# Two transformer blocks on one core: a planner that lets certain DVE and POOL instructions exclude each other, and convolution sums kept in PSUM

## The chip, the cores and the metric

The kernel runs on one core of a Trainium2 chip. The metric is the device time of the whole program in microseconds. The engines are named as in the profile: PE (TensorE, matrix products; PEld its weight loads), DVE (VectorE), ACT (ScalarE), POOL (GpSimd) and SP (SyncE, which issues the DMAs).

## The reference

Sequence of 512 tokens, width 1024, float32, batch 1. Two blocks follow each other, each with two layers:

```python
def first_block(x, ...):                       # twice:
    h = _rmsnorm(x, g_mix[l]); p = h @ w_in[l]
    # latent attention, 8 heads of 64+32, with rotary tables
    y_attn = _mla_attention(q_nope, q_rope, k_nope, k_rope, v)
    a, gt = jnp.split(p[..., o3:], 2, axis=-1)
    u = a * jax.nn.sigmoid(gt)                 # 512 channels
    u = _dwconv(u, w_dw_conv[l], b_dw_conv[l]) # 31 taps over the tokens
    u = jax.nn.silu(_layernorm(u, ...))
    x = x + jnp.concatenate([y_attn, u], axis=-1) @ w_o[l]
    z = _dwconv(_rmsnorm(x, g_ffn[l]) @ w_up[l], w_dw_ffn[l], b_dw_ffn[l])   # 3 taps
    zg, zv = jnp.split(z, 2, axis=-1)
    x = x + (jax.nn.silu(zg) * zv) @ w_down[l]
def second_block(x, p, ...):
    # layer 0: state space mixer; layer 1: gated linear recurrence; each followed by
    # layer norms, a squared-relu feed-forward (4096 wide) and an embedding gate
```

## The kernel before

Everything is kept transposed: a tile has 128 channels in its partitions and the 512 tokens in its columns, so x is eight tiles. Weights come from HBM in units (128 columns of eight row tiles are the usual one, 512 KB) into one of three buffers of class `r`. Each unit is split exactly into two float32r parts: `hi`, a cast that ACT or DVE makes, and `lo`, the remainder, a subtraction (`s<-r,s` in the profile) that DVE or POOL makes. An operand is split the same way, and each product is three float32r products (hi*hi, hi*lo, lo*hi) into a PSUM bank.

No order is written by hand. `record` runs through the program and only notes each operation with the tiles that it reads and writes; `schedule` then plays the core through with a cost for every operation (`cost`, `cost_tensor`) and latencies between engines, picks at each step the operation and the engine that can start first (ties by `prio`), and gives each tile a buffer; `issue` emits the instructions in that order. Each engine then works through its own list in order. Since all instructions are emitted by one line of `issue`, the profile gives all of them that line (L572 before). Tile classes stand in the profile's names: `psum` (eight banks), `s` (86 buffers of 2 KB a partition), `r` weights, `u` the padded inputs of the convolutions, `V` small vectors such as taps, `t` and `n` small tiles, `C` constants.

Some operations may go to either of two engines: `R.either` is POOL first, DVE second, `R.other` the reverse, `copy` ACT first, DVE second. In `schedule` the second choice pays `second` (2000) in the priority and is only considered if it would end no more than `eager` (500 ns) after the first. `KEEP` says how many buffers of a class an operation must leave for older operations that have yet to take theirs; for `psum` it is 2.

`mixer1` is the mixer of block 1: `in0`/`in1` (norm, projections, gates U, latents, rope tables in layer 0), then eight heads of attention and, after each second head, `conv_tile(j)` for one of four channel tiles, then the output projection. A convolution tile has 31 taps. DVE takes 17 of them, each one instruction U * tap + sum; for 14 taps (`SIDE_TAPS`) ACT makes the product and `R.either` adds it to a second sum; a last `R.either` addition joins the two:

```python
R.vector.scalar_tensor_tensor(conv[j], U[j][:, k:k + S], wc, conv[j], op0=ALU.mult, op1=ALU.add)
...
R.scalar.activation(t, U[j][:, k:k + S], AF.Identity, scale=vec(f"w_dw_conv{l}", j * CONV_K + k))
...
R.either.tensor_add(side, side, t)
...
R.either.tensor_add(conv[j], conv[j], side)
```

Of the kernel before, what the change touches and what calls it, by code (L numbers as in the profile page):

```python
# [14 lines left out]
ALU = mybir.AluOpType  # L15
# [23 lines left out]
# ---------------------------------------------------------------- weight units  # L39
def weight_units():  # L40
    """(name, layer, first row, row tiles, column pieces); a piece is (start, stop) or (None, zeros)."""
# [100 lines left out]
# ---------------------------------------------------------------- small vectors  # L142
def vec_layout():
    """name -> (first column, columns)"""
# [64 lines left out]
def constants():  # L209
    """[128, *] of 0 and 1: identity, s<=l, all ones, rope sum, two-way selector, level masks"""  # L210
# [19 lines left out]
# ---------------------------------------------------------------- recorded program and its schedule  # L230
class Tl:
    """A tile of the recorded program; its memory is chosen when the program is scheduled."""
# [11 lines left out]
class Ap:  # L244
    """An access pattern on a recorded tile: the steps to rebuild it and the elements it covers."""
# [68 lines left out]
class Op:  # L314
    __slots__ = ("i", "eng", "calls", "cost", "preds", "succs", "npred", "ready", "tiles", "start", "end", "prio", "label", "tab", "tail", "bias", "alts", "done")


class Recorder:
    """Takes the instructions in program order, orders them per engine by a simulation of the core, and issues them."""
# [8 lines left out]
    def __init__(self):  # L328
        self.ops, self.bias, self.label, self.switch = [], 0, "", 150
        self.greed, self.order_w, self.second, self.eager = 0.015, 1.0, 2000, 500  # L330
# [34 lines left out]

    def cost_tensor(self, calls):
        """A product streams its columns while the weights of the next one load."""
        stream, load = [], []
        for meth, args, kw in calls:
            n, m = args[0].n, args[1].n  # L370
            once = meth == "transpose" or args[1].tl.dt == F32R
            stream += [2.5 + n / 2.4] if once and meth != "transpose" else [2.5 + n / 1.2] * (1 if once else 2)
# [3 lines left out]
    def together(self, calls):  # L376
        """Products of the tensor engine that stay in one run."""
        self.add("tensor", "matmul", (), {}, [("matmul", a, k) for a, k in calls])

    def any(self, *forms):  # L380
        """One operation in several forms (engine, method, arguments, options); the schedule picks one."""
        eng, meth, args, kw = forms[0]
        self.add(eng, meth, args, kw)
        self.ops[-1].alts = [(e, self.cost(e, m, a, k), [(m, a, k)]) for e, m, a, k in forms]

# [1245 lines left out]
```

## Time and profile before

| | |
|---|---|
| time, median of 3 runs | 2938.12 us (2937.53 to 2942.33) |
| profiled execution | span 2940.1 us, first to last instruction, 2.0 us above that median; no other time of it is given |
| busy | PE 2778.7 us, DVE 2051.8, POOL 1459.2, ACT 1193.5 |
| DMA | 230.74 MB read, 79 GB/s over the span |
| mean granted clock of PE | 0.977 |

A row of a group gives what it writes and reads, the shape, the count, then busy us and mean ns of one instruction, then the engine's idle time before them and who ended it. A row of a stretch gives its length, then for PE, PEld, DVE, ACT and POOL the busy us (and instructions), the granted PE clock, the share of the DMA engines' time, and GB/s. A row of the timeline gives start, length, engine and instruction, merged over equal neighbours. A row of the waits gives who waited for whom: us in total, times, longest.

### The profile page before, as it was taken

The numbers are of one execution on the slowest core, as the hardware profiler recorded it, in microseconds if no ns is written. First come the engines' busy times: TensorE is split into PE (matmuls) and PEld (weight loads), VectorE is DVE, ScalarE is ACT, GpSimd is POOL, SyncE is SP. The second block draws the span as 40 slices with busy tenths as digits, with TensorE's granted clock in tenths as the row PEclk, the third lists the DMA queues.
The fourth block names the chain that finished last, engine by engine and source line by source line (L and its number), as shares of the span: only waits on it lengthen the run. The fifth ranks groups of instructions, "written<-read, shape, count | busy, mean of one in ns | idle before, by whom it ended". The sixth has DMA issues, their size and how long they took to land. (4 is left out here: it accounts for less than half of the span.)

```text
span 2940.1 us, 37496 instructions
## 1 busy us (share of the span) xinstructions
PE 2778.7 (95%) x14054; PEld 2283.6 (78%) x14054; DVE 2051.8 (70%) x2962; ACT 1193.5 (41%) x2162; POOL 1459.2 (50%) x1163
## 2 busy tenths in 40 slices
PE   7788999999788999999999999999989999899999
PEld 5566788888577888887667888888878788788888
DVE  8999777766998766675674665455687777745546
ACT  4585332335584332244553333122345563322223
POOL 5786434454875334462254563344564544434443
PEclk8899999999899999999999999999999999999999
DMA  4003213331013223331112422233231113223230
GB/s 161 13 24 122 72 65 108 115 126 35 9 58 115 72 100 94 102 108 37 37 44 79 124 70 95 92 106 109 64 94 44 51 51 99 75 93 108 94 108 30
DMA packets 69445, 235.26 MB, mean 80 GB/s; under 512 B 7824, under 2 KB 11024, under 8 KB 69264
## 3 DMA queue, kind: packets, MB, share of 16 engines
q1 hardware_dynamic: 69264, 232.87, 24.7%
q8 instruction: 111, 1.82, 0.2%
q14 instruction: 70, 0.57, 0.1%
HBM read 230.74 MB, written 2.10 MB: 79 GB/s over the span
## 5 line engine op out<-in xcount | busy, mean ns | idle before, releaser
L572 PE MATMUL psum<-s,s 128*128 128x512 f32 (+2 forms) x12752 | 2709.8, 370 | 73.1 <-DVE s L572 49.7
L572 PEld LDWEIGHTS psum<-s,s 128*128 128x128 f32 (+1 forms) x12752 | 2167.4, 190 | 521.8 <-DVE s L572 62.5
L572 POOL TENSOR_TENSOR s<-r,s 128x512 fp32r<-128x512 f32 (+1 forms) x632 | 894.1, 1434 | 903.6 <-ACT s L572 452.0
L572 POOL TENSOR_TENSOR s<-s,s 128x512 f32<-128x512 f32 (+4 forms) x395 | 468.3, 1201 | 379.0 <-DVE s L572 215.5
L572 ACT CAST s<-r 128x512 fp32r<-128x512 f32 (+1 forms) x681 | 385.4, 609 | 381.8 <-DMA r<-wts 340.1
L572 DVE TENSOR_TENSOR s<-s,s 128x512 fp32r<-128x512 f32 (+4 forms) x453 | 418.3, 935 | 84.9 <-ACT s L572 70.1
L572 DVE TENSOR_TENSOR s<-s,psum 128x512 f32<-128x512 f32 (+2 forms) x400 | 224.6, 590 | 284.0 <-PE psum L572 283.2
L572 DVE SCALAR_TENSOR_TENSOR s<-u,V,s 128x512 f32<-128x512 f32 x304 | 324.1, 1076 | 52.5 <-ACT s L572 49.1
L572 ACT ACTIVATE s<-s 128x512 f32<-128x512 f32 (+1 forms) x338 | 188.8, 578 | 281.5 <-DVE s L572 279.5
L572 ACT ACTIVATE s<-psum 128x512 f32<-128x512 f32 (+2 forms) x174 | 91.5, 527 | 453.3 <-PE psum L572 449.1
L572 ACT ACTIVATE s<-u,V 128x512 f32<-128x512 f32 x200 | 144.3, 760 | 258.2 <-DVE u L572 257.8
L572 DVE TENSOR_TENSOR s<-r,s 128x512 fp32r<-128x512 f32 (+1 forms) x237 | 235.7, 1010 | 12.9 <-ACT s L572 9.3
L572 PE MATMUL psum<-C,s 128*128 128x128 f32 (+1 forms) x500 | 93.2, 282 | 53.2 <-POOL s L572 26.4
L572 DVE SCALAR_TENSOR_TENSOR s<-psum,s 128x512 f32<-128x512 f32 (+1 forms) x88 | 55.7, 638 | 112.1 <-ACT s L572 112.1
L572 DVE CAST s<-r 128x512 fp32r<-128x512 f32 (+1 forms) x188 | 101.3, 554 | 42.3 <-DMA r<-wts 42.2
L572 PEld LDWEIGHTS psum<-C,s 128*128 128x128 f32 x500 | 66.3, 157 | 73.0 <-POOL s L572 27.9
L572 DVE CAST s<-s 128x512 fp32r<-128x512 f32 (+1 forms) x105 | 105.8, 1008 | 8.1 <-POOL s L572 2.9
L572 DVE TENSOR_TENSOR u<-psum,s 128x512 f32<-128x512 f32 x88 | 60.5, 687 | 71.1 <-PE psum L572 70.7
L572 ACT CAST s<-s 128x512 fp32r<-128x512 f32 (+2 forms) x110 | 63.4, 587 | 99.8 <-DVE s L572 86.8
L572 ACT ACT_TABLE_LOAD x70 | 89.8, 1283 | 17.7 <-DVE s L572 14.2
L572 DVE SCALAR_TENSOR_TENSOR s<-psum,V,s 128x511 f32<-128x511 f32 (+4 forms) x90 | 66.4, 745 | 38.7 <-ACT s L572 32.9
L572 DVE TENSOR_TENSOR s<-psum,s 128x512 fp32r<-128x512 f32 (+3 forms) x131 | 84.8, 678 | 3.8 <-PE psum L572 2.1
(85 smaller groups left out, 1052.7 us busy)
## 6 DMA issues: line engine op xcount, KB each, us to landing
r<-wts SPq DMA_DIRECT2D x415, 512.0 KB, 3.6
r<-wts SPq DMA_DIRECT2D x12, 256.0 KB, 2.7
r<-wts SPq DMA_DIRECT2D x8, 384.0 KB, 3.0
s<-xT SPq DMA_DIRECT2D x8, 256.0 KB, 5.8
s<-pT SPq DMA_DIRECT2D x8, 256.0 KB, 4.0
outT<-s SPq DMA_DIRECT2D x16, 128.0 KB, 1.7
r<-wts SPq DMA_DIRECT2D x9, 128.0 KB, 2.1
V<-vecs SPq DMA_DIRECT2D x1, 480.5 KB, 6.7
```

What stands on the lines that cost most here:

```text
L572: getattr(eng, meth)(*[res(a) for a in args], **{k: res(v) for k, v in kw.items()})
```

## The change

Five things change in the planner and one in the program.

- `shares` marks operations that the planner from now on treats as needing one common port: every POOL operation, and DVE operations with two large inputs outside PSUM, or a copy or tensor_scalar from and to SBUF. `schedule` starts a marked operation no earlier than the end of the last marked one (`port`).
- The rule for the second engine is replaced: `second` and `eager` are 0, and an operation on the slower of its engines is counted as starting later by half the difference of the two costs (`drag`).
- A float32r product of n columns is planned at 2.5 + n/2.28 ns, before 2.5 + n/2.4.
- `KEEP["psum"]` is 4, before 2.
- The running sum of a convolution tile is a PSUM bank, and the last addition is always DVE's, from that bank to SBUF.
- Comments and docstrings are gone, so line numbers differ (`issue` emits at L590 now).

```diff
-        self.greed, self.order_w, self.second, self.eager = 0.015, 1.0, 2000, 500
+        self.greed, self.order_w, self.second, self.eager, self.drag = 0.015, 1.0, 0, 0, 0.5
...
+    @staticmethod
+    def shares(eng, meth, args, kw):
+        if eng != "vector":
+            return eng == "gpsimd"
+        out = kw["out"] if "out" in kw else args[0]
+        ins = list(args if "out" in kw else args[1:]) + [v for n, v in kw.items() if n not in ("out", "accum_out")]
+        near = sum(isinstance(a, Ap) and a.n > 1 and a.tl.cls != "psum" for a in ins)
+        if meth in ("tensor_scalar", "tensor_copy"):
+            return near == 1 and out.tl.cls != "psum"
+        return near > 1
...
-            stream += [2.5 + n / 2.4] if once and meth != "transpose" else [2.5 + n / 1.2] * (1 if once else 2)
+            stream += [2.5 + n / 2.28] if once and meth != "transpose" else [2.5 + n / 1.2] * (1 if once else 2)
...
-                    s = max(t0, s)
+                    s = max(t0, s, port) if o.shared[p] else max(t0, s)
...
+                    s += self.drag * ([x[1] for x in o.alts if x[0] == p][0] - min(x[1] for x in o.alts))
                     key = (s, o.prio + (self.switch if load else 0) + (self.second if p != o.alts[0][0] else 0), o.i)
...
+                if o.shared[p]:
+                    port = o.end
...
-KEEP = {"psum": 2, "s": 18, "u": 2, "t": 6, "n": 16}
+KEEP = {"psum": 4, "s": 18, "u": 2, "t": 6, "n": 16}
...
         def conv_tile(j):
             R.label = f"conv{l}"
+            acc = bank()
             for k in range(CONV_K - SIDE_TAPS):
                 wc = vec(f"w_dw_conv{l}", j * CONV_K + k)
                 if k == 0:
-                    R.vector.tensor_scalar(conv[j], U[j][:, 0:S], wc, vec(f"b_dw_conv{l}", j), op0=ALU.mult, op1=ALU.add)
+                    R.vector.tensor_scalar(acc, U[j][:, 0:S], wc, vec(f"b_dw_conv{l}", j), op0=ALU.mult, op1=ALU.add)
                 else:
-                    R.vector.scalar_tensor_tensor(conv[j], U[j][:, k:k + S], wc, conv[j], op0=ALU.mult, op1=ALU.add)
+                    R.vector.scalar_tensor_tensor(acc, U[j][:, k:k + S], wc, acc, op0=ALU.mult, op1=ALU.add)
...
-                R.either.tensor_add(conv[j], conv[j], side)
+            R.vector.tensor_add(conv[j], acc, side)
```

The change reorders the whole program, so three places of the new order are shown. In the program as a whole POOL has 1163 instructions before and 714 after, DVE 2962 and 3370, ACT 1996 and 2037 (without table loads and the like). Of the subtractions `s<-r,s` with 512 columns, POOL has 618 before and 357 after, DVE 230 and 491.

The start of the convolution of layer 0 on DVE; `u2` and `u0` are inputs of two channel tiles, `V0` holds the taps. Before:

```order
L572 SCALAR_TENSOR_TENSOR s52_623<-u2_71,V0_65,s52_623 128x512
L572 SCALAR_TENSOR_TENSOR s62_629<-u0_67,V0_65,s62_629 128x512
L572 SCALAR_TENSOR_TENSOR s52_623<-u2_71,V0_65,s52_623 128x512
L572 SCALAR_TENSOR_TENSOR s62_629<-u0_67,V0_65,s62_629 128x512
L572 SCALAR_TENSOR_TENSOR s52_623<-u2_71,V0_65,s52_623 128x512
L572 SCALAR_TENSOR_TENSOR s68_775<-psum1_658,V0_65,s70_766 128x512
```

and after:

```order
L590 SCALAR_TENSOR_TENSOR psum2_617<-u2_71,V0_65,psum2_617 128x512
L590 TENSOR_SCALAR psum0_877<-u0_67,V0_65 128x512
L590 SCALAR_TENSOR_TENSOR psum2_617<-u2_71,V0_65,psum2_617 128x512
L590 SCALAR_TENSOR_TENSOR psum0_877<-u0_67,V0_65,psum0_877 128x512
L590 TENSOR_SCALAR n5_899<-psum7_883 128x4
L590 SCALAR_TENSOR_TENSOR s83_904<-psum5_747,V0_65,s50_893 128x512
L590 SCALAR_TENSOR_TENSOR psum2_617<-u2_71,V0_65,psum2_617 128x512
L590 SCALAR_TENSOR_TENSOR psum0_877<-u0_67,V0_65,psum0_877 128x512
```

The sums are in banks 2 and 0, two at a time, and instructions of the latents and the attention stand between the steps that before stood in a block.

The first subtractions of weights on POOL, ahead of its part of the first norm (`n3_531`, `n2_515`: a power of four columns). Before:

```order
L572 TENSOR_TENSOR s84_461<-r1_406,s81_450 128x512
L572 TENSOR_TENSOR s28_480<-r2_424,s5_472 128x512
L572 TENSOR_TENSOR s33_514<-r0_465,s31_507 128x512
L572 TENSOR_TENSOR n3_531<-n2_523,n0_74 128x4
L572 TENSOR_TENSOR s38_545<-r0_465,s9_505 128x512
```

and after:

```order
L590 MEMSET u3_80 128x15 x2
L590 ISA
L590 TENSOR_TENSOR n2_515<-n1_505,n0_74 128x4
L590 TENSOR_TENSOR s41_544<-r2_448,s34_480 128x256
L590 TENSOR_TENSOR s43_551<-r0_466,s38_490 128x256
```

Nothing but memsets stands ahead of the power on POOL now; the subtractions are on DVE.

The same norm on DVE: `n2_523` and `n1_505` are made from the sums that PE left in bank 7; `s54`, `s55` and `s62`, `s63` belong to the rope tables. Before:

```order
L572 TENSOR_SCALAR s55_299<-s55_299 128x512
L572 TENSOR_SCALAR s54_295<-s54_295,V0_65 128x512
L572 CAST s31_507<-r0_465 128x512
L572 SCALAR_TENSOR_TENSOR s11_512<-s83_456,V0_65,s54_295 128x512
L572 TENSOR_SCALAR s55_299<-s55_299,V0_65 128x512
L572 TENSOR_SCALAR n2_523<-psum7_509 128x4
```

and after:

```order
L590 SCALAR_TENSOR_TENSOR s62_332<-s66_348,s62_332 128x512
L590 SCALAR_TENSOR_TENSOR s63_338<-s78_403,s63_338 128x512
L590 TENSOR_SCALAR n1_505<-psum7_498 128x4
L590 SCALAR_TENSOR_TENSOR s62_332<-s77_398,s62_332 128x512
L590 SCALAR_TENSOR_TENSOR s63_338<-s33_473,s63_338 128x512
L590 TENSOR_TENSOR n3_528<-n2_515 128x4
```

Before, nearly all of the rope tables' work stood ahead of the norm; now part of it stands behind.

More of the change, by code (lines that the diff above doesn't have):

```diff
@@ L314 @@
 class Op:
-    __slots__ = ("i", "eng", "calls", "cost", "preds", "succs", "npred", "ready", "tiles", "start", "end", "prio", "label", "tab", "tail", "bias", "alts", "done")
+    __slots__ = ("i", "eng", "calls", "cost", "preds", "succs", "npred", "ready", "tiles", "start", "end", "prio", "label", "tab", "tail", "bias", "alts", "done", "shared")
 class Recorder:
@@ L384, in any @@
         self.ops[-1].alts = [(e, self.cost(e, m, a, k), [(m, a, k)]) for e, m, a, k in forms]
+        self.ops[-1].shared = {e: self.shares(e, m, a, k) for e, m, a, k in forms}
     def add(self, eng, meth, args, kw, calls=None):
@@ L392, in add @@
             o.alts = [(e, self.cost(e, meth, args, kw), calls) for e in self.EITHER.get(eng, (eng,))]
+        o.shared = {e: eng != "tensor" and self.shares(e, meth, args, kw) for e, _, _ in o.alts}
         eng = o.alts[0][0]
@@ L471, in schedule @@
         order = []
-        table, loads = None, 0
+        table, loads, port = None, 0, 0.0
         while n < len(ops):
@@ L522, in schedule @@
             (s, _, _), o, p = best
+            o.eng, o.cost, o.calls = [x for x in o.alts if x[0] == p][0]
+            s -= self.drag * (o.cost - min(x[1] for x in o.alts))
             o.start = s
-            o.eng, o.cost, o.calls = [x for x in o.alts if x[0] == p][0]
             for e, _, _ in o.alts:
@@ L960, in conv_tile @@
                 if k == 0:
-                    R.vector.tensor_scalar(conv[j], U[j][:, 0:S], wc, vec(f"b_dw_conv{l}", j), op0=ALU.mult, op1=ALU.add)
+                    R.vector.tensor_scalar(acc, U[j][:, 0:S], wc, vec(f"b_dw_conv{l}", j), op0=ALU.mult, op1=ALU.add)
                 else:
-                    R.vector.scalar_tensor_tensor(conv[j], U[j][:, k:k + S], wc, conv[j], op0=ALU.mult, op1=ALU.add)
-            if SIDE_TAPS:
-                side = None
-                for k in range(CONV_K - SIDE_TAPS, CONV_K):
-                    t = tl()
-                    R.scalar.activation(t, U[j][:, k:k + S], AF.Identity, scale=vec(f"w_dw_conv{l}", j * CONV_K + k))
-                    if side is None:
-                        side = t
-                    else:
-                        R.either.tensor_add(side, side, t)
-                R.either.tensor_add(conv[j], conv[j], side)
+                    R.vector.scalar_tensor_tensor(acc, U[j][:, k:k + S], wc, acc, op0=ALU.mult, op1=ALU.add)
+            side = None
+            for k in range(CONV_K - SIDE_TAPS, CONV_K):
+                t = tl()
+                R.scalar.activation(t, U[j][:, k:k + S], AF.Identity, scale=vec(f"w_dw_conv{l}", j * CONV_K + k))
+                if side is None:
+                    side = t
+                else:
+                    R.either.tensor_add(side, side, t)
+            R.vector.tensor_add(conv[j], acc, side)
         att = [pair() for _ in range(4)]
```

## Prediction, made before the changed kernel ran

> **What bounds the kernel now.** I read the page's first block, then the busy time of stretches of the span, because the average hides that the limit changes from stage to stage.
>
> ```profile
> span 2940.1 us, 37496 instructions
> ...
> PE 2778.7 (95%) x14054; PEld 2283.6 (78%) x14054; DVE 2051.8 (70%) x2962; ACT 1193.5 (41%) x2162; POOL 1459.2 (50%) x1163
> ```
>
> ```profile
> core 0: us, PE busy (x) PEld busy (x) DVE busy (x) ACT busy (x) POOL busy (x), PEclk, DMA share, GB/s
> 50.00:250.00 200.00, 146.62 (x710) 116.96 (x710) 198.58 (x277) 133.10 (x257) 155.81 (x114) 0.90 0.11 37
> 350.00:700.00 350.00, 350.00 (x1534) 287.59 (x1533) 237.15 (x285) 107.77 (x178) 151.31 (x113) 1.00 0.28 95
> 705.00:925.00 220.00, 189.37 (x873) 151.32 (x872) 211.91 (x297) 150.45 (x286) 164.57 (x122) 0.91 0.16 51
> 950.00:1250.00 300.00, 300.00 (x1314) 246.64 (x1313) 204.85 (x252) 89.38 (x143) 116.51 (x80) 1.00 0.29 92
> 2150.00:2500.00 350.00, 323.38 (x2363) 283.43 (x2362) 258.20 (x403) 180.68 (x340) 172.46 (x158) 0.97 0.21 65
> ```
>
> 350 to 700 and 950 to 1250 are the feed-forward layers of block 1: PE is never idle, DVE has 30% left. No order of instructions makes them shorter, since PE's own rate sets it (1093 products in 250.6 us, 0.229 us each):
>
> ```profile
> L572 PE MATMUL psum<-s,s 128*128 128x512 f32 x1093 | 250.6, 392 | 0.0
> ```
>
> 50 to 250 and 705 to 925 are the two mixers with attention and the 31-tap convolution. There DVE is busy 198.6 of 200 and 211.9 of 220 us, PE idles 53.4 and 30.6 us. So DVE sets the time of these 420 us, and what DVE does in them is the question. Its groups in the two mixers (the first four rows from 50 to 250, the last three from 705 to 875), and behind them groups of the whole span that read PSUM:
>
> ```profile
> L572 DVE SCALAR_TENSOR_TENSOR s<-u,V,s 128x512 f32<-128x512 f32 x64 | 78.2, 1258 | 0.0
> L572 DVE CAST s<-r 128x512 fp32r<-128x512 f32 x15 | 12.1, 823 | 0.0
> L572 DVE TENSOR_TENSOR s<-s,s 128x512 f32<-128x512 f32 x9 | 11.1, 1240 | 0.0
> L572 DVE TENSOR_TENSOR s<-r,s 128x512 fp32r<-128x512 f32 x7 | 6.2, 890 | 0.0
> ...
> L572 DVE SCALAR_TENSOR_TENSOR s<-u,V,s 128x512 f32<-128x512 f32 x64 | 72.2, 1139 | 0.2
> L572 DVE TENSOR_SCALAR s<-u,V 128x512 f32<-128x512 f32 x4 | 5.0, 1256 | 0.0
> L572 DVE TENSOR_SCALAR s<-u,V 128x512 f32<-128x512 f32 x4 | 5.0, 1263 | 0.0
> ```
>
> ```profile
> L572 DVE TENSOR_TENSOR s<-s,psum 128x512 f32<-128x512 f32 x256 | 169.2, 681 | 241.2 <-PE psum L572 240.6
> L572 DVE SCALAR_TENSOR_TENSOR s<-s,V,psum 128x512 f32<-128x512 f32 x32 | 22.8, 743 | 15.9 <-PE psum L572 15.0 <-POOL s L572 0.8
> ...
> L572 DVE SCALAR_TENSOR_TENSOR s<-psum,V,s 128x511 f32<-128x511 f32 x24 | 17.9, 748 | 33.0 <-ACT s L572 32.9
> ```
>
> A convolution step (U times a tap plus the running sum, both in SBUF) takes 1.258 us, the same form with one operand in PSUM 0.743. The timeline tells why. DVE's and POOL's rows around 90 and 108 us:
>
> ```profile
> 88.68 15.38 DVE L572 SCALAR_TENSOR_TENSOR s<-u,V,s 128x512 f32<-128x512 f32 x9
> 108.31 4.05 DVE L572 SCALAR_TENSOR_TENSOR s<-u,V,s 128x512 f32<-128x512 f32 x6
> ...
> 89.87 15.32 POOL L572 TENSOR_TENSOR s<-s,s 128x512 f32<-128x512 f32 x9
> 113.08 0.13 POOL L572 MEMSET u<- 128x1 f32 x2 [7.89 <-DVE s L572]
> ```
>
> While POOL adds, nine steps take nine POOL times (1.71 us each); while POOL stands still (the 7.89 us before 113.08), six take 4.05 us, 0.675 each. The two engines alternate: an instruction of the one runs only when that of the other is through. DVE instructions with a PSUM operand show no trace of it.
>
> **The change, part by part.** (a) The running sums move to PSUM. 64 steps in each mixer leave the alternation. No row has DVE writing a 512-column PSUM tile, so the price is bounded: below by the 0.675 of a step without POOL, above by the 1.258 of now (no gain at all). I take 0.675, since the nearest rows (0.743 and 0.748, durations that overlap the next instruction by some 0.07, as six of 0.74 fit into 4.05) show no surcharge for a PSUM input. Layer 0: 64 x (1.258 - 0.675) = -37.3 us of DVE. Layer 1: 64 x (1.139 - 0.675) = -29.7. The first step of a tile (TENSOR_SCALAR, 1.26) gives 4 x 0.58 = -2.3 in each.
>
> [...]
>
> (b) Fewer instructions on POOL. Counted in the program, POOL goes from 1163 to 714 and DVE from 2962 to 3370; the mixer of layer 0 has 136 on POOL before and 95 after, 358 and 399 on DVE; that of layer 1 137 and 113, 316 and 333. What goes over is mostly the second half of the weight split (s<-r,s). Alone on DVE it takes 0.68 us, less the overlap 0.61, and a cast 0.42:
>
> ```profile
> 55.04 0.68 DVE L572 TENSOR_TENSOR s<-r,s 128x512 fp32r<-128x512 f32 x1
> ...
> 59.84 0.42 DVE L572 CAST s<-r 128x512 fp32r<-128x512 f32 x1
> ```
>
> Layer 0: 41 x 0.61 = 25 us more for DVE, of which some 20 in the stretch where it is full (before 50 us DVE has idle time: the 41 include the splits of the first weights). Layer 1: 17 x 0.61 = +10.4.
>
> (c) With less on POOL, the other DVE instructions wait less. Layer 0, by the rows above: casts 15 x (823 - 420) = 6.0 us, adds 9 x (1240 - 680) = 5.0, splits 7 x 0.21 = 1.5; -12.5 at most. Layer 1 has 12 such adds, -6.7. POOL still has 95 and 113 instructions, so I count three quarters: -9.4 and -5.0.
>
> (d) PE's waits. In 50 to 250 it waited 31.2 us for POOL and 15.4 for DVE:
>
> ```profile
> PE psum L572 <- POOL s L572: 17.8, 3, 16.6
> PE psum L572 <- DVE s L572: 15.4, 13, 3.6
> PE psum L572 <- POOL n L572: 13.4, 1, 13.4
> ```
>
> The 13.4 ends at 63.66: all banks hold products that wait for the row factor of the first norm; its DVE part (62.25, in n<-psum) stood behind the angle reduction of the rope tables. The 16.6 ends at 117.13, a sum on POOL behind the adds above.
>
> ```profile
> 44.59 9.59 DVE L572 SCALAR_TENSOR_TENSOR s<-s,s 128x512 f32<-128x512 f32 x14
> 62.25 0.15 DVE L572 TENSOR_SCALAR n<-psum 128x4 f32<-128x4 f32 x1
> ...
> 63.66 1.11 PE L572 MATMUL psum<-C,n 128*128 128x128 f32 x4 [13.44 <-POOL n L572]
> 117.13 0.59 PE L572 MATMUL psum<-C,s 128*128 128x1 f32 x2 [16.63 <-POOL s L572]
> ```
>
> Both lie within the stretch that DVE fills and are how its lateness reaches PE; they are not added. In the new order the norm's instruction stands ahead of a dozen of the rope's, the convolution is spread between the attention's instructions, and the side adds remain on POOL, so both waits should shrink by more than half.
>
> (e) The rest. PE's price in the planner (512 columns: 227 ns, before 216) agrees with the 0.229 above and makes no product faster. The feed-forward stages take 46 more DVE instructions in layer 0, 46 x 0.61 = 28 us into the 113 that DVE has free there: nothing. ACT gets 39 more casts, 39 x 0.6 = 24 us at 41% busy: nothing. The recurrence (2150 to 2500) is a chain of DVE and PE; DVE gets 78 more instructions (29 of 0.61, the rest, mostly of 256 columns, about 0.37: +36 us) and loses waits, by the first three rows below against 412 for 256 columns (the fourth, which reads PSUM) and 680 for 512: 64 x 0.40 + 57 x 0.24 + 31 x 0.36 = -50 at most.
>
> ```profile
> L572 DVE TENSOR_TENSOR s<-s 128x256 f32<-128x256 f32 x64 | 48.8, 811 | 0.0
> L572 DVE TENSOR_TENSOR s<-s,s 128x256 f32<-128x256 f32 x57 | 35.8, 655 | 1.1 <-POOL s L572 0.9
> L572 DVE TENSOR_TENSOR s<-r,s 128x512 fp32r<-128x512 f32 x31 | 31.8, 1038 | 1.9 <-ACT s L572 1.5
> ...
> L572 DVE TENSOR_TENSOR s<-s,psum 128x256 f32<-128x256 f32 x128 | 46.7, 412 | 23.7 <-PE psum L572 23.5
> ...
> L572 ACT CAST s<-r 128x512 fp32r<-128x512 f32 (+1 forms) x681 | 385.4, 609 | 381.8 <-DMA r<-wts 340.1
> 130.00:250.00 120.00, 98.54 (x517) 78.25 (x517) 118.95 (x186) 88.76 (x180) 102.64 (x78) 0.97 0.12 42
> ```
>
> With three quarters of that it is a wash: 0, between -15 and +15.
>
> Sum: layer 0: -37.3 - 2.3 + 20 - 9.4 = -29.0. Layer 1: -29.7 - 2.3 + 10.4 - 5.0 = -26.6. Together -55.6, so 2940.1 - 55.6 = 2884.5 for the profiled execution. Its span stands 2.0 above the median of the runs (2938.1); the forecast is 2882.5, rounded 2883.
>
> **Rivals.** *PE takes over at once, larger gain.* If spreading the convolution ends DVE's lateness altogether, both stretches shrink to PE's busy time: 53.4 + 30.6 = 84, 2854; and the clock there (0.90, 0.91) would be granted in full as in the stages without holes, up to 10% of the 336 busy us, so down to about 2830. For: ACT and POOL have room. Against: DVE still needs some 170 of 200 us in each, and attention goes back and forth.
>
> *The banks run out, slower.* An accumulator holds one of eight banks for 17 steps, and two are open at once (order on DVE, above); six are left. The planner now keeps four for older work, up from two, so a later head can start only with five free. From the point where just one half-head is in flight, each of its four visits to DVE queues behind a convolution step: 16 x 4 x 0.675 = 43 us a layer against the 28 gained, +15 each, about 2968. For: attention already fills 130 to 250 us (the last row above) with DVE at 118.95. Against: in the new order PE's rows of the attention still change between several heads' tiles, as before. [...]
>
> *PSUM writes are slow.* At the upper end of (a) the 39.6 and 32.0 us are lost, and the sum is -55.6 + 71.6 = +16: 2954.
>
> *No change.* What DVE saves on waits (12.5 + 39.6 in layer 0) it gives back on moved work and new stalls; then 2938. It needs moved work to cost double (41 x 1.26 = 52), the price it has only beside a busy POOL.
>
> **How the numbers follow.** Forecast 0.56, larger gain 0.25, no change 0.06, slow PSUM writes 0.03, banks 0.10. A difference of 0.2% (6 us) is about what can be told from no change here. Faster 0.81, same 0.06, slower 0.13. The range takes in the larger gain down to 2832 and, upward, losing half the sum (2910) and a recurrence 15 us worse (2925); left out are most of the last three cases, 0.19.
>
> **What would show it.** Right: convolution steps at 0.74 us whatever POOL does; POOL near 900 us busy, DVE's s<-r,s mean below 0.85; feed-forward starting some 29 us earlier in layer 0 and 56 in layer 1; PE's waits for POOL before 250 us under 15. Wrong: steps above 0.9 us; PE idle within the feed-forward stages; attention stretches longer than 120 us, PE waiting for DVE in them; the time from 2150 to 2500 growing.

## The result and the profile after

The changed kernel takes 2814.4 us (median; 2811.9 to 2816.2), the one before, run beside it, 2939.8: a ratio of 0.957 (95% interval 0.956 to 0.959), 125 us less. The direction was predicted, the size was not: 2883 was forecast, and 2814 lies below the range. The first block of the page of after:

```profile
span 2814.0 us, 37098 instructions
...
PE 2745.5 (98%) x14054; PEld 2259.6 (80%) x14054; DVE 1923.5 (68%) x3370; ACT 1215.0 (43%) x2201; POOL 837.1 (30%) x714
```

PE is now busy for all but 68 us of the span, against 161 before, and its products are 33 us shorter in sum, while the granted clock rose from 0.977 to 0.993. DVE does 408 more instructions in 128 us less.

Where the time went, by stages of the program. A stage begins with the first product of it in the trace (matched to the order of products in the program), so the rows of one column can be compared, although nothing in the trace is labelled. "ssd" is the state space mixer and "recurrence" the gated linear one; ff is each stage's feed-forward (with gate and tail). One profiled execution each, us:

| kernel | mixer 0 | ff 0 | mixer 1 | ff 1 | ssd | ff, gate | recurrence | ff, tail |
|---|---|---|---|---|---|---|---|---|
| before | 296.8 | 367.8 | 258.0 | 377.1 | 436.5 | 422.9 | 342.5 | 438.6 |
| after | 259.2 | 366.1 | 233.0 | 368.3 | 425.1 | 422.3 | 307.5 | 432.5 |
| difference | -37.6 | -1.7 | -25.0 | -8.9 | -11.3 | -0.6 | -34.9 | -6.1 |

Half of the gain is in the two mixers of block 1 (-62.6), where it was predicted (-55.6, though two of its terms were off in opposite directions, as is told below). A second large piece is in the recurrence, for which 0 was predicted. The busy time of stretches of after, columns as in the prediction; the first and third are the mixers, the second and fourth their feed-forward, the last is the recurrence:

```profile
50.00:250.00 200.00, 175.01 (x841) 136.65 (x842) 189.34 (x328) 158.99 (x298) 128.77 (x107) 0.97 0.18 61
259.00:625.00 366.00, 366.00 (x1593) 298.10 (x1592) 245.48 (x360) 124.58 (x202) 66.70 (x56) 1.00 0.29 99
667.00:858.00 191.00, 177.37 (x858) 140.97 (x857) 174.59 (x309) 152.82 (x289) 122.39 (x104) 0.97 0.19 59
858.00:1227.00 369.00, 367.67 (x1650) 301.45 (x1648) 251.25 (x391) 126.97 (x211) 62.59 (x47) 1.00 0.30 99
2074.00:2381.00 307.00, 304.99 (x2331) 271.88 (x2330) 233.06 (x469) 186.29 (x352) 85.29 (x77) 1.00 0.22 71
```

From 50 to 250 us PE gets through 841 products where it did 710, at a clock of 0.97 instead of 0.90, and DVE is still nearly full (189 of 200): the mixers have become shorter, not another kind of stage. In the recurrence it is otherwise: PE is busy 305.0 of 307 us. Before, its whole stretch was

```profile
2159.00:2501.00 342.00, 315.38 (x2331) 277.04 (x2331) 250.48 (x398) 176.86 (x332) 165.54 (x155) 0.97 0.20 62
```

26.6 us of holes, and 10.4 us more for the same 2331 products at the lower clock. All but 2.0 us of holes is gone, 35 us together.

DVE's groups of after from 50 to 250 us (two rows), from 667 to 858 (the next) and in the whole span:

```profile
L590 DVE SCALAR_TENSOR_TENSOR psum<-u,V,psum 128x512 f32<-128x512 f32 x64 | 47.3, 742 | 0.3
L590 DVE TENSOR_TENSOR s<-s,s 128x512 f32<-128x512 f32 x18 | 15.9, 882 | 0.7 <-ACT s L590 0.7
...
L590 DVE SCALAR_TENSOR_TENSOR psum<-u,V,psum 128x512 f32<-128x512 f32 x64 | 45.7, 742 | 0.1
...
L590 DVE TENSOR_TENSOR s<-r,s 128x512 fp32r<-128x512 f32 x491 | 346.9, 733 | 5.4 <-ACT s L590 3.5
```

A convolution step takes 0.742 us (1.258 and 1.139 before) while POOL is busy 129 and 122 us of these stretches. What PE waited for from 50 to 250 us, and where the two waits stand that the prediction named:

```profile
PE psum L590 <- ACT s L590: 12.6, 18, 2.1
PE psum L590 <- DVE s L590: 10.0, 10, 2.3
PE psum L590 <- POOL n L590: 2.6, 1, 2.6
```

```profile
50.56 0.65 PE L590 MATMUL psum<-C,n 128*128 128x128 f32 x4 [2.59 <-POOL n L590]
```

Of 31.2 us waiting for POOL, 2.6 are left. The first norm's factor comes at 50.56 instead of 63.66, and the wait of 16.6 us for a sum on POOL no longer exists.

### The profile page after: what moved, and what is told of

It is laid out like the page before. It is cut to its first block, busy times and chain, and to the rows that moved or that the text cites. A ratio compares the mean times of both kernels' runs of the same rounds, so it can differ in the third digit from the quotient of the medians.

```text
span 2814.0 us, 37098 instructions
## 1 busy us (share of the span) xinstructions
PE 2745.5 (98%) x14054; PEld 2259.6 (80%) x14054; DVE 1923.5 (68%) x3370; ACT 1215.0 (43%) x2201; POOL 837.1 (30%) x714
## 4 chain that ended last, share of the span: by engine, by line
PE 82%; DVE 13%; issue 3%; ACT 2%; POOL 0%; DMA 0%; DVEq 0%; POOLq 0%; ACTq 0%; SPq 0%
PE psum L590 82%; DVE s L590 9%; DVE psum L590 2%; ACT s L590 2%; DVE n L590 1%; ACT L590 0%; DMA r<-wts 0%; POOL s L590 0%; DVE u L590 0%; POOL n L590 0%; POOL u L590 0%; DVEq L590 0%; POOLq L590 0%; ACTq L590 0%; SPq L590 0%
## 5 line engine op out<-in xcount | busy, mean ns | idle before, releaser
L590 PE MATMUL psum<-s,s 128*128 128x512 f32 (+3 forms) x12752 | 2676.4, 368 | 36.5 <-DVE s L590 22.4
L590 PEld LDWEIGHTS psum<-s,s 128*128 128x128 f32 (+1 forms) x12752 | 2147.8, 188 | 480.1 <-DVE s L590 38.7
L590 POOL TENSOR_TENSOR s<-r,s 128x512 fp32r<-128x512 f32 (+1 forms) x370 | 498.0, 1363 | 1085.0 <-ACT s L590 696.0
L590 ACT CAST s<-r 128x512 fp32r<-128x512 f32 (+1 forms) x708 | 404.2, 610 | 374.1 <-DMA r<-wts 353.5
L590 DVE TENSOR_TENSOR s<-s,s 128x512 f32<-128x512 f32 (+5 forms) x610 | 402.4, 679 | 78.9 <-ACT s L590 68.4
L590 DVE TENSOR_TENSOR s<-s,psum 128x512 f32<-128x512 f32 (+2 forms) x400 | 224.5, 591 | 309.8 <-PE psum L590 309.3
L590 POOL TENSOR_TENSOR s<-s,s 128x512 f32<-128x512 f32 (+5 forms) x230 | 265.0, 1163 | 571.2 <-DVE s L590 352.5
L590 DVE TENSOR_TENSOR s<-r,s 128x512 fp32r<-128x512 f32 (+1 forms) x499 | 349.9, 728 | 5.4 <-ACT s L590 3.5
L590 ACT ACTIVATE s<-s 128x512 f32<-128x512 f32 (+1 forms) x338 | 187.7, 578 | 233.5 <-DVE s L590 230.9
L590 ACT ACTIVATE s<-psum 128x512 f32<-128x512 f32 (+2 forms) x174 | 91.7, 528 | 412.2 <-PE psum L590 409.6
L590 ACT ACTIVATE s<-u,V 128x512 f32<-128x512 f32 x200 | 142.9, 761 | 274.1 <-DVE u L590 273.8
L590 DVE SCALAR_TENSOR_TENSOR s<-u,V,s 128x512 f32<-128x512 f32 x176 | 146.1, 831 | 49.4 <-ACT s L590 47.1
L590 DVE SCALAR_TENSOR_TENSOR s<-psum,s 128x512 f32<-128x512 f32 (+1 forms) x88 | 55.6, 639 | 119.1 <-ACT s L590 119.1
L590 DVE TENSOR_TENSOR u<-psum,s 128x512 f32<-128x512 f32 x88 | 60.6, 689 | 89.1 <-PE psum L590 89.1
L590 PE MATMUL psum<-C,s 128*128 128x128 f32 (+1 forms) x500 | 87.1, 277 | 19.1 <-ACT s L590 14.2
L590 ACT CAST s<-s 128x512 fp32r<-128x512 f32 (+2 forms) x121 | 70.6, 592 | 64.7 <-DVE s L590 63.7
L590 DVE CAST s<-r 128x512 fp32r<-128x512 f32 (+1 forms) x161 | 68.7, 441 | 39.3 <-DMA r<-wts 39.3
L590 DVE TENSOR_TENSOR s<-psum,s 128x512 fp32r<-128x512 f32 (+4 forms) x139 | 90.7, 679 | 7.0 <-ACT s L590 6.4
L590 POOL TENSOR_TENSOR n<-n,n 128x4 f32<-128x4 f32 (+1 forms) x32 | 34.4, 1076 | 204.7 <-DVE n L590 204.4
L590 DVE SCALAR_TENSOR_TENSOR psum<-u,V,psum 128x512 f32<-128x512 f32 x128 | 93.0, 742 | 0.5
L590 PEld LDWEIGHTS psum<-C,s 128*128 128x128 f32 x500 | 61.3, 149 | 36.1 <-ACT s L590 22.4
## 6 DMA issues: line engine op xcount, KB each, us to landing
r<-wts SPq DMA_DIRECT2D x12, 256.0 KB, 2.8
s<-xT SPq DMA_DIRECT2D x8, 256.0 KB, 6.0
s<-pT SPq DMA_DIRECT2D x8, 256.0 KB, 4.0
```

Of the source, the lines that this page charges most:

```text
L590: getattr(eng, meth)(*[res(a) for a in args], **{k: res(v) for k, v in kw.items()})
```

## The experiments

Times are medians against the kernel before in the same runs, with the ratio's interval. Stages in us, of one profiled execution each:

| run | time | ratio (95%) | mixer 0 | mixer 1 | ssd | recurrence |
|---|---|---|---|---|---|---|
| before | 2939.8 | 1 | 296.8 | 258.0 | 436.5 | 342.5 |
| after | 2814.4 | 0.957 (0.956 to 0.959) | 259.2 | 233.0 | 425.1 | 307.5 |
| e1 PSUM sums alone | 2886.9 | 0.982 (0.980 to 0.984) | 272.6 | 235.4 | 436.9 | 342.1 |
| e2 rule alone | 2947.3 | 1.003 (1.002 to 1.004) | 305.0 | 270.4 | 435.2 | 340.1 |
| e3 rule and port | 2855.6 | 0.971 (0.970 to 0.973) | 280.8 | 251.4 | 428.9 | 304.4 |
| e4 all but PSUM | 2853.8 | 0.971 (0.969 to 0.972) | 272.0 | 256.0 | 426.5 | 306.8 |
| e5 rule, POOL priced dear | 2904.1 | 0.988 (0.986 to 0.990) | 286.7 | 268.4 | 438.7 | 316.3 |
| e6 all but the port | 2910.7 | 0.991 (0.989 to 0.992) | 291.8 | 254.0 | 436.7 | 333.3 |
| e7 port, not in recurrence | 2841.6 | 0.967 (0.965 to 0.968) | 259.9 | 232.0 | 425.2 | 335.6 |
| e8 port with old rule | 2928.7 | 0.996 (0.995 to 0.998) | 312.2 | 262.3 | 438.9 | 309.2 |
| e9 old price and KEEP | 2826.8 | 0.961 (0.960 to 0.963) | 267.1 | 234.8 | 429.3 | 304.4 |
| e10 after, repeated | 2813.9 | 0.957 (0.956 to 0.958) | 259.5 | 230.5 | 425.1 | 307.5 |
| e11 10 side taps | 2812.9 | 0.957 (0.955 to 0.958) | 257.5 | 234.2 | 426.1 | 306.9 |
| e12 18 side taps | 2828.9 | 0.962 (0.961 to 0.964) | 264.6 | 241.9 | 427.1 | 306.6 |
| e13 before, recurrence on DVE | 2892.3 | 0.984 (0.983 to 0.986) | 297.3 | 257.1 | 436.9 | 305.9 |
| e14 after, other ties | 2823.7 | 0.961 (0.960 to 0.963) | 262.1 | 234.7 | 430.9 | 309.4 |
| e15 before, other ties | 2913.6 | 0.992 (0.990 to 0.993) | 290.3 | 261.1 | 434.5 | 335.1 |
| e16 after, chains on DVE | 2829.4 | 0.962 (0.961 to 0.964) | 258.5 | 233.1 | 437.9 | 305.0 |

The last rows set the measure for the others: any edit of the planner reorders the whole program, and e14 and e15 show what a mere reordering is worth.

### e14, e15: what chance in the order is worth

The weight that settles near ties (`greed`) is 0.0152 instead of 0.015, in after and in before; nothing else changes.

```diff
-        self.greed, ... = 0.015, ...
+        self.greed, ... = 0.0152, ...
```

> A control: the full change with a tie-breaking weight of the planner moved by 1.3% (greed 0.0152 for 0.015), which reorders thousands of instructions for no reason. The difference to 2814 is the planner's scatter: within 10 us, single stages within 8 us.

> The same control on the kernel before. Within 15 us of 2938: the old plan knows less of what happens, so its scatter may be larger. If the kernel before was merely an unlucky order: 2910 or less.

After becomes 9 us slower, before 26 us faster, which is more than the 15 that were expected. So before had a somewhat unlucky order, and up to some 26 us of the 125 can't be put down to a part of the change. Each of the two is one sample, so they give a size and no bound: a total that differs by less than 9 us from a kernel planned with the port, or by less than 26 us from one planned without it, may be chance. A difference in one stage below some 10 us is read only where several runs agree (e15's largest are -7.4 in the recurrence and -6.5 in mixer 0).

### e10: a repeat

`switch` 160 instead of 150, meant as a second sample of such chance.

> A control: the full change with one number of the planner that should not matter (the priority that a table load costs, 160 for 150). Whatever it differs from 2814 is the planner's scatter, against which the other differences must be read: within 6 us by both theories, each stage within 4 us.

It gave the same order on every engine, so it is the changed kernel once more: 2813.9 us. It says nothing of chance in the order, but how well a time repeats (0.5 us).

### e1: the sums in PSUM and nothing else

```diff
+            acc = bank()
...
-                    R.vector.scalar_tensor_tensor(conv[j], U[j][:, k:k + S], wc, conv[j], ...)
+                    R.vector.scalar_tensor_tensor(acc, U[j][:, k:k + S], wc, acc, ...)
...
-                R.either.tensor_add(conv[j], conv[j], side)
+                R.vector.tensor_add(conv[j], acc, side)
```

> The kernel before with one part of the change: the convolution's running sums in PSUM and its last addition on DVE; the planner is the old one. Theory A (the gain is DVE time of the mixers, mostly the convolution steps that leave the alternation with POOL): steps at 0.74 us, 67 us less DVE work in the two mixers, the time falls by 40 to 65 us, to 2875 to 2900; the recurrence stays at 342 us. Theory B (work that leaves POOL frees the other DVE instructions everywhere, the PSUM sums matter little): 2920 or more. Theory C (the banks run out): above 2940.

52 us less, 47 of them in the mixers (-24.2, -22.6), against 67 us of DVE work that was expected to go there; recurrence, ssd and gate don't move. DVE's steps from 50 to 250 us:

```profile
L572 DVE SCALAR_TENSOR_TENSOR psum<-u,V,psum 128x512 f32<-128x512 f32 x64 | 44.8, 745 | 0.0
```

and a stretch of that mixer in e1:

```profile
50.00:225.00 175.00, 139.35 (x669) 110.76 (x668) 169.97 (x274) 134.82 (x262) 133.22 (x114) 0.91 0.14 47
```

0.745 us a step, though POOL is busy 133 of 175 us here, with the old rule and no port in the plan. DVE's and POOL's rows of e1 around 80 us show it best:

```profile
76.39 10.62 DVE L572 SCALAR_TENSOR_TENSOR psum<-u,V,psum 128x512 f32<-128x512 f32 x16
...
78.67 10.36 POOL L572 TENSOR_TENSOR s<-s,s 128x512 f32<-128x512 f32 x8
```

Sixteen steps run on end at 0.66 us each and eight of POOL's additions beside them at 1.30, where before nine of each took turns at 1.71. So it is the place of the sum that takes the step out of the alternation, not the new order, and writing PSUM costs no more than the 0.675 of a step in SBUF while POOL stands still.

### e4: all but the sums in PSUM

The changed kernel, with the convolution as before (sums in SBUF, last addition on either engine; the diff of e1 reversed).

> The full change without the PSUM sums (running sums in SBUF again, last addition on either engine). Theory A: the mixers lose what they won, 50 to 65 us more than 2814: 2865 to 2880, and the recurrence stays at 307. Theory B: the sums are a small part, 2830 or less.

2853.8, between the two theories: the sums are worth 39 us on top of the rest (mixers -12.8 and -23.0, from 272.0 and 256.0). That is less than the 52 alone. The steps, in SBUF here (from 50 to 272 us, then from 640 to 895), show why:

```profile
L590 DVE SCALAR_TENSOR_TENSOR s<-u,V,s 128x512 f32<-128x512 f32 x64 | 56.1, 881 | 0.0
...
L590 DVE SCALAR_TENSOR_TENSOR s<-u,V,s 128x512 f32<-128x512 f32 x64 | 57.9, 916 | 0.0
```

Without any help from PSUM they have come down from 1258 and 1139 ns (the same form takes 1125 and 1105 ns in e2, with the rule alone, and 904 and 820 in e3, with the port). The port in the plan has already brought part of what the sums bring; in mixer 0 the whole stage is 24.8 us shorter than before without them.

### e2, e3: the rule alone, and the rule with the port

From before, e2 takes only the new rule for the second engine (`second` 0, `eager` 0, `drag` 0.5); e3 takes this and `shares` with the port. Both keep the sums in SBUF, the price 2.5 + n/2.4 and KEEP 2.

```diff
-        ..., self.second, self.eager = ..., 2000, 500
+        ..., self.second, self.eager, self.drag = ..., 0, 0, 0.5
...                                           (e3 only, and `shares`:)
-                    s = max(t0, s)
+                    s = max(t0, s, port) if o.shared[p] else max(t0, s)
```

> The kernel before with the new rule for the second engine alone (second 0, eager 0, drag 0.5): sums in SBUF, no port in the plan, old price of products, KEEP 2. Theory B: some 400 instructions go from POOL to DVE, the two-input means on DVE fall towards 0.7 us, the recurrence falls from 342 to about 310 us, the whole to 2860 to 2890. Theory A: without a place for the convolution steps DVE stays full in the mixers, and the time changes by less than 20 us. Theory D (only an order that keeps the two engines apart helps, moving work alone does not): 2920 to 2950.

> The kernel before with the rule and the port in the plan, sums in SBUF, old price of products, KEEP 2. Theory B: like the run with the rule alone, within 15 us. Theory D: at least 20 us below the run with the rule alone, the recurrence at about 307 us. Beside the full change (2814) it lacks the PSUM sums, which by theory A are worth 50 us: 2865.

The rule alone is 8 us slower; the port makes 92 us of difference (2947 to 2856), -24 and -19 in the mixers, -36 in the recurrence. The page's first block of e2, and DVE's group of the weight split in its whole span:

```profile
PE 2780.3 (94%) x14054; PEld 2283.5 (78%) x14054; DVE 2040.9 (69%) x3040; ACT 1207.9 (41%) x2177; POOL 1357.8 (46%) x1071
```

```profile
L590 DVE TENSOR_TENSOR s<-r,s 128x512 fp32r<-128x512 f32 x233 | 213.9, 935 | 4.3 <-ACT s L590 0.9
```

The same two of e3:

```profile
PE 2760.0 (97%) x14054; PEld 2270.3 (80%) x14054; DVE 1974.6 (69%) x3418; ACT 1227.4 (43%) x2221; POOL 780.7 (27%) x650
```

```profile
L590 DVE TENSOR_TENSOR s<-r,s 128x512 fp32r<-128x512 f32 x513 | 371.0, 749 | 6.4 <-ACT s L590 4.6
```

With the rule, 92 instructions leave POOL, not the 400 that theory B expected; with the port 421 more. DVE then does 378 instructions more than in e2 in 66 us less, because they are shorter on average: the same subtraction takes 0.749 instead of 0.935 us. Both times are those of theory D; the rule's +8 is less than chance in the order can do.

### e6: all but the port

```diff
-                    s = max(t0, s, port) if o.shared[p] else max(t0, s)
+                    s = max(t0, s)
```

> The full change with the port alone taken out of the plan. POOL has 1075 instructions, 149 of them in the recurrence as before (150). Theory B and theory D alike: the PSUM sums stay (-52), the rule stays (+8), the recurrence goes back to 342 us: 2885 to 2905. If the port in the plan only pays in the company of SBUF sums: 2820 to 2840.

2910.7, 96 us slower than after and 6 above the range expected: +33 and +21 in the mixers, +12 in ssd, +26 in the recurrence (by the profiled execution, which took 2916.5). From the other side this gives nearly the same price for the port as e3 against e2. Without it, the new rule, price and KEEP make the kernel of e1 24 us slower, not faster, which is still within the 26 that chance did in e15.

### e5: off POOL, but not apart

The port does two things: it moves work from POOL to DVE, and it plans what is left at times when the other engine has no marked operation planned. e5 does the first without the second: e2 with POOL's two-input instructions priced 2.2 times dearer.

```diff
-            return 147 + 2.105 * n
+            return 2.2 * (147 + 2.105 * n)
```

> The new rule alone (as in the second run), with POOL's two-input operations priced 2.2 times as dear in the plan: no port, sums in SBUF, old price of products, KEEP 2. POOL keeps 664 instructions, as many as with rule and port (646), but nothing in the plan keeps the two engines apart. Theory B (what pays is that work leaves POOL): within 15 us of the run with rule and port (2856), the recurrence at 315 us or less. Theory D (the plan must keep the two engines apart in time): 2900 or more, the recurrence at 335 or more.

The page's first block and the group of the split again, of e5:

```profile
PE 2781.7 (96%) x14054; PEld 2284.9 (79%) x14054; DVE 2070.5 (71%) x3447; ACT 1202.8 (41%) x2171; POOL 872.8 (30%) x668
```

```profile
L590 DVE TENSOR_TENSOR s<-r,s 128x512 fp32r<-128x512 f32 x457 | 355.3, 802 | 6.8 <-ACT s L590 4.6
```

As many instructions on POOL as in e3 (668 and 650), yet 2904 against 2856. So moving alone brings 43 of the 92 us (2947 to 2904), planning apart the other 48, both more than e15's 26. POOL's instructions are longer than in e3: its additions of 512 columns take 1.75 us against 1.47, all 668 of its instructions 872.8 us against 780.7 for 650. The dearer price also lets the plan believe that POOL is busy for longer than it is, so a part of the 48 may be a plan that fits less well; no run separates this. The total is theory D's, but the recurrence all but theory B's: there the moving does most (340.1 to 316.3, with 304.4 in e3).

### e8: apart, but on POOL

The reverse: the port in the plan with the old rule (2000, 500, no `drag`), which prefers POOL; sums in SBUF, price 2.5 + n/2.4, KEEP 4.

```diff
-        self.second, self.eager, self.drag = 0, 0, 0.5
+        self.second, self.eager, self.drag = 2000, 500, 0.0
```

> The port in the plan with the old rule for the second engine; sums in SBUF, old price of products, KEEP 4 (with 2 the plan finds no bank). The old rule now sends more to POOL: 1490 instructions on it, 183 in the recurrence, but planned apart from DVE's. Theory B: work on POOL costs, so slower than before: 2960 to 3050, the recurrence above 350. Theory D: the order counts, so faster than before: below 2920, two-input means on DVE at 0.8 us or less.

The page's first block of e8, and the stretch of its recurrence:

```profile
PE 2794.0 (95%) x14054; PEld 2288.2 (78%) x14054; DVE 1582.8 (54%) x2433; ACT 1295.1 (44%) x2360; POOL 1831.8 (63%) x1494
```

```profile
2181.00:2490.00 309.00, 305.31 (x2334) 271.70 (x2333) 196.91 (x332) 196.16 (x372) 208.00 (x194) 1.00 0.23 72
```

POOL has 194 instructions in the recurrence, more than before (155), and PE is busy 305 of 309 us all the same. So a POOL instruction there does no harm as such; one at the wrong moment does. But mixer 0 gets 15 us longer (312.2; mixer 1 with 262.3 is within chance), so the total lies between the two theories. DVE is busy 203 and POOL 192 of the 262 us from 50 to 312, so neither is full, and what holds the mixer there is not shown. In the whole the port and the rule each bring no more than chance, and 84 us together (e3).

### e7: the port everywhere but in the recurrence

```diff
-                    s = max(t0, s, port) if o.shared[p] else max(t0, s)
+                    s = max(t0, s, port) if o.shared[p] and not o.label.startswith("hg") else max(t0, s)
```

> The full change, but the plan ignores the port for the operations of the recurrence (labels hg_in, hg_core, hg_out), which keep 151 on POOL there. If the 35 us of the recurrence come from its own operations: the recurrence at 335 to 345 us, the whole at 2842 to 2852, all other stages as in the full change within 3 us. If they come from a better start (earlier loads, bank order): 2815 to 2825.

27 us slower than after, and all of it in the recurrence: it takes 335.6 us instead of 307.5, every other stage is within 1.5 us of after. The stretch, and DVE's 256-column additions in it:

```profile
2073.00:2409.00 336.00, 314.56 (x2338) 276.70 (x2338) 248.79 (x416) 179.61 (x339) 159.11 (x153) 0.97 0.20 65
```

```profile
L590 DVE TENSOR_TENSOR s<-s 128x256 f32<-128x256 f32 x55 | 35.0, 683 | 0.0
```

### e13: the kernel before, the recurrence off POOL

The opposite edit: before, where operations labelled `hg_` that may go to either engine go to DVE only. The planner has no port.

```diff
-            o.alts = [... for e in self.EITHER.get(eng, (eng,))]
+            o.alts = [... for e in (("vector",) if eng in self.EITHER and self.label.startswith("hg_") else self.EITHER.get(eng, (eng,)))]
```

> The kernel before, old planner, no port, sums in SBUF; only in the recurrence (labels hg_) all operations that may go to POOL or DVE go to DVE: POOL keeps 16 of 150 there, DVE has 477 instead of 355. If the waits for POOL on DVE's part of the chain are the cost: the recurrence at 305 to 318 us though DVE gets some 60 us more work in it, the whole at 2905 to 2918. If DVE's sum of work counts, as the prediction reckoned (+60 us of work against 65 us of waits): 335 to 345 us, the whole at 2930 to 2945. If only an order that is planned around the port helps: above 330.

47 us less, 37 of it in the recurrence, which takes 305.9 us as with the whole change, and 9 in the tail; mixers and ssd stay within 1 us. The recurrence is where the first theory put it; the whole is 13 us below its range, nearly all of that by the tail, for which no run gives a cause.

The stretch of the recurrence in e13, and DVE's same additions in it:

```profile
2155.00:2460.00 305.00, 303.30 (x2329) 271.14 (x2329) 234.64 (x502) 181.60 (x344) 38.72 (x38) 1.00 0.23 71
```

```profile
L572 DVE TENSOR_TENSOR s<-s 128x256 f32<-128x256 f32 x80 | 29.5, 415 | 0.0
```

DVE does 104 more instructions there than before (502 and 398) and is busy 16 us less. The mean of this one form goes with the length of the stage. The row of the same group in after is

```profile
L590 DVE TENSOR_TENSOR s<-s 128x256 f32<-128x256 f32 x67 | 28.2, 464 | 0.0
```

and the stage takes 342.5 us at 811 ns (before, shown in the prediction), 335.6 at 683 (e7), 307.5 at 464 (after), 305.9 at 415 (e13). e8 falls a little out of line (309.2 at 554, by the same view), but there DVE has only 332 instructions.

What PE waited for in the recurrence, before:

```profile
PE psum L572 <- DVE s L572: 16.1, 11, 3.5
PE psum L572 <- ACT s L572: 10.3, 8, 2.8
```

and the one row of these that is left in after:

```profile
PE psum L590 <- DVE s L590: 1.7, 3, 0.8
```

### e16: the chains on DVE alone

After, where operations of the recurrence, the layer norms and ssd that may go to either engine go to DVE only (labels beginning with hg, ln, ss; the edit of e13).

> The full change with all operations that may go to POOL or DVE kept on DVE in the recurrence, the state space mixer and the layer norms (POOL 549 instructions instead of 710). If waits for POOL still cost there: 2795 to 2808, mostly in the state space mixer (425) and the tail. If these stages are at PE's rate or at their chains' latency now: within 10 us of 2814, which is the planner's scatter.

15 us slower than after: the recurrence gains 2.5, ssd loses 12.8 (a little more than chance in the order), so e13's cure does not carry over to every stage. DVE's subtractions in ssd, after and e16:

```profile
L590 DVE TENSOR_TENSOR s<-r,s 128x512 fp32r<-128x512 f32 x54 | 39.3, 761 | 0.6 <-ACT s L590 0.2
```

```profile
L590 DVE TENSOR_TENSOR s<-r,s 128x512 fp32r<-128x512 f32 x94 | 61.3, 685 | 1.5 <-ACT s L590 1.3
```

Each is shorter by 0.08 us, but there are 40 more of them, 22 us, and PE waits 13.8 us for DVE in ssd where it waited 2.6. The total fits neither theory.

### e9: the price of a product and KEEP as before

After with 2.5 + n/2.4 and KEEP 2.

```diff
-            stream += [2.5 + n / 2.28] ...
+            stream += [2.5 + n / 2.4] ...
...
-KEEP = {"psum": 4, ...
+KEEP = {"psum": 2, ...
```

> The full change with two of its numbers put back: the price of a product (n/2.4) and KEEP 2 for PSUM. If price and KEEP matter little (the run without PSUM sums lost 40 us with them as without them): within 10 us of the full change, 2805 to 2825. If keeping four banks back costs the attention (the rival of the banks): 2800 or less. If the honest price of products is what makes the plan fit: 2835 or more.

12 us slower, 8 of them in mixer 0: the two settings help by little more than chance in the order can do, 2 us above the range expected if they matter little (without PSUM sums, e4 against e3, they are worth 2). Neither pair shows that four banks kept for older work cost anything; a cost below chance can't be seen.

### e11, e12: another share of side taps

After with `SIDE_TAPS` 10 and 18 instead of 14, so that DVE takes 21 or 13 of the 31 taps.

```diff
-SIDE_TAPS = 14
+SIDE_TAPS = 10      (e12: 18)
```

> The full change with 10 of 31 taps on ACT and POOL instead of 14, so 21 on DVE, into PSUM. If DVE still sets the mixers (189 of 200 us busy in layer 0): 16 steps more, 10.8 us of DVE in each layer, less what 16 additions on POOL held it up: slower, 2820 to 2835. If POOL's additions are what holds the mixers: faster, 2800 to 2812.

> The full change with 18 of 31 taps on ACT and POOL, so 13 on DVE. If DVE sets the mixers: faster by 5 to 10 us, 2804 to 2810, while ACT (159 of 200 us) gets 10 us more in each layer. If ACT or POOL take over: 2815 to 2835.

With 10 the time is the same within its interval, which neither theory had; with 18 it is 14.5 us longer (+5.4 and +8.9 in the mixers), a little more than chance; four more additions a tile are planned through the port there. No version beats the changed kernel by more than chance.

## Why the sum for the mixers came out near and the forecast was wrong

**(a) Convolution steps: the price right, their worth not.** 0.742 us while POOL is busy, in the changed order and in the old one (e1); on end 0.66 (e1), so the 0.675 that the sum took stands. Reading and writing PSUM shows no surcharge: sixteen steps that do both take 10.62 us (e1), 0.66 each, no more than the 0.675 of one in SBUF while POOL stands still. But the sum booked 39.6 and 32.0 us for the two mixers. Alone the PSUM sums brought 24.2 and 22.6 (e1), on top of the rest 12.8 and 23.0 (e4 against after).

**(b) and (c) Moved work and other waits: the direction of each right, their sum wrong.** POOL is busy 837 us, `s<-r,s` takes 0.733 us. In mixer 0 the two-input additions on DVE went from 1240 to 882 ns, 64% of the way to 680, where three quarters were counted; the few splits from 50 to 250 us did not get shorter (890 and 927 ns). In all the two terms charged 10.6 and 5.4 us to the mixers. Matched to the planner's order, DVE's instructions of mixer 0 outside the convolution are 33 more and take 10.8 us less (179.3 before, 168.5 after, worked out from the traces, overlaps counted once), those of mixer 1 are 11 more and take 11.1 less. And e4, which has all of the change but the PSUM sums, is 24.8 us shorter in mixer 0 and 2.0 in mixer 1. So an order planned around the port is worth more than the moved work costs.

**(d) Waits of PE for POOL: right,** 2.6 us left of 31.2. They were not added to the sum; whether they should have been, no run separates. Feed-forward begins 37.6 us earlier in layer 0 (29 forecast) and 64.3 in layer 1 (56). That the mixers together gave -62.6 against -55.6 is luck in part: in mixer 0 (a) was booked some 15 to 27 us too high and (b) with (c) some 35 too low, more than chance in the order does to a stage. In mixer 1 the differences are within it. (The last of the three rows that the prediction gives for 705 to 875 us, with 1263 ns, is of 50 to 250 us; nothing hangs on it.)

**(e) The recurrence: wrong, and the step that failed.** The term was "0, between -15 and +15"; it measured -35. I had added up DVE's busy time, moved work against lost waits, and found a wash; in fact it fell from 250.5 us to 233.1. That is not the main fault: in a stage where DVE is busy 73% of the time its busy time is not the limit, so that sum says nothing on the length. PE and DVE take turns there (PE waited 16.1 us for DVE), and DVE's instructions that are longer beside POOL (811 ns before, 415 in e13, for the addition of 256 columns) are on the way to the next product: PE's own row showed 26.6 us of holes and a clock of 0.97, which for the same products bounds the gain at some 36 us. Nearly all of it was realised. That the time they lose beside POOL is the cause is shown from both sides: taking the port out of the plan for this stage alone brings the time back (e7, +28), and taking the work off POOL in the kernel before removes it (e13, -37), though DVE gets 104 instructions more. Against the rival that POOL's own slower instructions (`s<-s,s` of 256 columns: 921 ns before, DVE's 655) make the chain long speaks e8: 194 of them in the stage, planned apart, and 309.2 us. Mere reordering moved this stage by 7.4 us (e15), far less.

**What the sum left out.** The rest of the 70 us that were missed is -11 in ssd, -9 in ff 1, -6 in the tail, -7 in the mixers and -2 elsewhere. The prediction did not look at ssd at all. Its stretch before and after:

```profile
1300.00:1736.00 436.00, 429.64 (x2111) 327.03 (x2111) 271.07 (x498) 185.31 (x306) 193.59 (x159) 0.99 0.21 65
...
1227.00:1652.00 425.00, 419.54 (x2108) 322.09 (x2107) 282.13 (x548) 184.64 (x307) 127.36 (x109) 1.00 0.21 66
```

PE's holes there were 6.4 us and are 5.5, so what went is 10.1 us of PE's busy time for nearly the same products; the clock went from 0.99 to 1.00, and how much of it that is, is not shown. The stage is 7 to 11 us shorter in every kernel that has the new rule and the port together (e3, e4, e7, e9, e11, e12), and not in those without (e2, e5, e6), which speaks for the port; but e14 has -6 and e16 +1 with both, and a mere reordering moves stages by up to 7, so its size is not settled. That of ff 1 and the tail stays open: e15 has -6 and -5 there, so chance alone could do it.

**The rivals.** "PE takes over at once" did not come true where it was put: in the mixers DVE is still busy 189 of 200 us and PE idle for 25. Its mechanism shows in the recurrence, where PE now sets the time (305.0 of 307 us at full clock). Had the rival been asked of every stage with holes, it would have had its 35 us there. "PSUM writes are slow" is refuted by e1 (0.66 us a step on end). "The banks run out" did not happen: the attention of layer 0, with accumulators open beside it, takes 120 us from its first product to its last, as before (97 to 217 us; 98.55 us of products now, 98.54 then), and KEEP 2 is no faster (e9). "No change" needed moved work at double cost; over the whole span it came at 0.73, against 0.68 alone.

```profile
97.00:217.00 120.00, 98.55 (x506) 75.58 (x505) 116.87 (x219) 100.68 (x205) 92.21 (x78) 0.97 0.19 63
```

**The change as a whole.** The four changes of the planner and the one of the program, in the order before, rule, port, price and KEEP, PSUM: 2939.8, 2947, 2856, 2854, 2814. The port brings 92 in company of the rule, the sums 39 (52 alone). The steps of 8 and 2 are within chance.

## What to carry to other kernels

Where two engines alternate, ask of each stage whose turn the next one waits for: in a chain between PE and DVE longer DVE instructions can lengthen the stage even when DVE is a quarter idle (one addition 811 against 415 ns, the recurrence 342.5 against 305.9 us), and for the same products an estimate of the most to gain is PE's holes plus what the granted clock would give back (26.6 and some 10 us there, 35 measured). Before costing moved work by busy time, look whether that engine fills the stage; if not, work moved onto it can be free, as in e13 (104 instructions more on DVE, the stage 37 us shorter), though not everywhere (e16, ssd 12.8 us longer). Where a sum comes out near, check its terms one by one: here e1 and e4 did, and two of them were wrong in opposite directions. Let a planner know which instructions of two engines were measured to take turns (nine steps of DVE and nine additions of POOL, 1.71 us each) and let it choose the engine freely: either alone was worth +8 or -11 us here, no more than chance, both together -84.

## What was not expected of the hardware

- A DVE instruction that reads and writes its sum in the same PSUM bank takes 742 to 745 ns beside a busy POOL, no more than one that only reads PSUM (743).
- An order alone keeps two engines apart: apart from the data that they hand on, nothing in the program makes DVE wait for POOL, and yet planned times hold well enough on the chip. Summed over all DVE instructions, the time above the duration that the same form has when undisturbed (taken to be its 8th percentile in the same trace; worked out from the traces) fell from 533 us in before to 191 in after. With the sums in SBUF and nearly equal work on POOL it is 212 with the port (e3) and 308 without (e5). DVE's steps with both inputs in SBUF (`s<-u,V,s`, 512 columns, over the whole span of before) took 1.29 us where POOL was busy for over a tenth of their time (185 of 304, worked out from the trace) and 0.75 elsewhere.
- Where PE's holes shrank, the granted clock rose: 53.4 to 25.0 us of 200 and 0.90 to 0.97 in mixer 0, 30.6 of 220 to 13.6 of 191 and 0.91 to 0.97 in mixer 1, 26.6 to 2.0 and 0.97 to 1.00 in the recurrence. Ten of the 35 us there are products at the higher clock (315.4 us busy for 2331 of them before, 305.0 after).
